# A two-layer GLA / attention / S5 trunk step: layer 1's S5 constants computed during layer 0, and attention's q, k, v passed through DRAM

## The chip, the cores and the metric

The kernel runs on one NeuronCore of one Trainium2 chip. The metric is device time in microseconds for one launch, less is better. TensorE is called PE below, VectorE DVE, ScalarE ACT, GpSimd POOL, and SyncE (which issues the DMAs of this kernel) SP.

## The reference

Two layers run on 640 tokens: 128 context tokens and 512 latent tokens, 1024 channels wide, all in fp32. Each layer has three branches that read the same normalised input: gated linear attention (GLA), latent attention (MLA) and an S5 state-space model. Their outputs are gated, projected, mixed and added to the residual. What matters here is cut from the reference:

```
# S5: the constants depend on weights alone
dt = exp(log_dt); mag = exp(a_re*dt); ab = mag*(cos(a_im*dt) + i sin(a_im*dt))
coef = (ab - 1) / (a_re + i a_im)
ub = coef * einsum('blgp,gnp->blgn', u, b)          # 32 groups, 64 states, 2 directions
x  = complex_linear_scan(ab, ub, x0)
y  = d_skip*u + Re(einsum('blgn,gpn->blgp', x, c))
# MLA: 4 heads, 96 = 64 + 32 rotary
q = rope(rms_norm(rms_norm(cq) @ w_uq));  k = rope(rms_norm(concat(ckv @ w_uk, k_rope)));  v = ckv @ w_uv
latent tokens attend to 256 cached + 512 latent tokens, context tokens to the 128 context tokens
o = softmax(q k^T / sqrt(96)) v
```

## The kernel before, in words

**Products.** Every large product is made of three fp32r matmuls (high x high, high x low, low x high). A weight half of 128x512 comes by DMA into `wraw`, ACT rounds it into `whi` and DVE subtracts to get `wlo` (`half`, L255; the copies are recorded at L227, the subtraction at L236, all matmuls at L245); each of the three tiles has 4 buffers. Projections go to the PSUM tile `pj`, all else to `bank` (4 buffers).

**Order.** PE runs strictly in the order in which the program is written. The other engines and the DMA queue on SP are put in order ahead of time by a scheduler that has a priority for each instruction; at run time each engine follows its own list and waits at the first row that is not ready. So an instruction of low priority, once it has a place in the list, holds back whatever stands behind it.

**Fill.** Projections that nothing waits for yet stand ready as generators in `self.stand`. `fill(n)` takes n steps from them; one step is six matmuls of 320 columns on 128x128 weights (four with `whi`, two with `wlo`). Fill is called where PE would otherwise wait. When `stand` is empty, `fill` does nothing.

**One layer** (`layer`, L1480) runs: S5 kernel, S5 input and `s5_z`, `s5_pow`, `s5_scan`, `s5_y`, `s5_glu`, then `mla_qkv`, `mla_heads`, then GLA, merges and output projection.

**S5's constants.** `s5_prep` (L632) makes from the weights the powers `s5pw`, the input coefficients `s5w` and the step `s5ab`: some 120 small DVE instructions. `s5_kernel` (L732) then makes 16 tiles `s5qk` of 128x512 by `outer` (L712: two products and a sum, recorded at L716, L717 and L718), stores each to DRAM (`qd`, L756) for use in `s5_y` (L947), and multiplies them with `s5rd`; `s5_z` makes 16 tiles `s5r` in the same way (its transposes are at L825); `s5_pow` (L856) doubles the powers in four rounds. Each round of `s5_pow` is followed by four fill steps:

```
for _ in self.s5_pow(p):
    fill(FILL[3])          # FILL[3] = 4
for _ in self.s5_scan(p):
    fill(FILL[3])
```

For layer 1, `s5_prep` and the first parts of `s5_kernel` stand at the end of layer 0 and the start of layer 1.

**Attention.** `mla_qkv` (L1077) makes k in 7 token tiles, v in 7 and q in 5. For each tile of k and q, ACT squares and copies the product out of PSUM, DVE reduces (`hss`), POOL raises to the power -1/2 (`hrs`), DVE scales each of four heads (L1133, L1165) and applies the rotation (L1065 to L1068). The results stay in the SBUF tiles `qt`, `kt`, `vt` for all heads. `mla_heads` (L1169) then transposes a head's part of q and k on PE (`load`, transposes at L1183), splits v (`values`), and runs scores, softmax, transposes of P (L1236) and the product with v for the query groups A and B (256 latent tokens each) and C (the 128 context tokens). The first head's transposes follow `mla_qkv` and ten fill steps.

Of the kernel before, what the change touches and what calls it, by code (L numbers as in the profile page):

```python
# [19 lines left out]
L = 2  # L20
# [164 lines left out]
FILL = (17, 2, 1, 4, 2, 10, 10, 1, 7, 3)  # L185
FM = (1, 6, 1, 4, 2, 4, 3, 2, 1)
# [15 lines left out]
class Prog:  # L202
# [113 lines left out]
    def consts(self):  # L316
# [20 lines left out]
        self.qd = [self.dr.tile([8, 2, 128, 512], F32, name=f"qd{l}") for l in range(L)]  # L337
        self.sud = [self.dr.tile([NT, 512], F32, name=f"sud{l}") for l in range(L)]
# [246 lines left out]
    def cmul(self, V, p, o_r, o_i, ar, ai, br, bi, shape):  # L585
        pat = "p (a b) -> p a b"
        t1 = p.tile([128, shape[1] * shape[2]], F32, name="cm1", tag="cm1")
        t2 = p.tile([128, shape[1] * shape[2]], F32, name="cm2", tag="cm2")
        t1, t2 = (t.rearrange(pat, a=shape[1]) for t in (t1, t2))
# [26 lines left out]
    def exp_(self, V, p, out, x):  # L616

        t = p.tile([128, 3, 64], F32, name="ex", tag="ex")
        k, r, y = t[:, 0], t[:, 1], t[:, 2]
# [8 lines left out]
        e = p.tile([128, 64], I32, name="exi", tag="exi")  # L628
# [3 lines left out]
    def s5_prep(self, l, vec, p, pz, ptmp):  # L632

        V = self.V
        n0 = VEC["B1"][0]
        bs, cs = pz.tile([128, 1024], F32, name="s5b"), p.tile([128, 1024], F32, name="s5c")
        with self.tc.high_priority(5200):
            for i, t in enumerate((bs, cs)):
                self.S.dma_start(t, self.a["vec"][l][:, n0 + 1024 * i:n0 + 1024 * i + 1024])
        self.B1, self.B2, self.C1, self.C2 = (t[:, 512 * i:512 * i + 512].rearrange("p (g c) -> p g c", c=16)  # L640
                                              for t in (bs, cs) for i in range(2))
        are, aim, ldt = vec("are"), vec("aim"), vec("ldt")
        sm = ptmp.tile([128, 11, 64], F32, name="s5sm")
# [33 lines left out]
        pw = p.tile([128, 9, 2, 64], F32, name="s5pw")  # L677
# [32 lines left out]
        self.pw, self.w, self.ab = pw, w, ab  # L710
# [21 lines left out]
    def s5_kernel(self, l, vec, p):  # L732
# [3 lines left out]
        V.tensor_scalar(c0, self.C1, self.nsgn, None, op0=ALU.mult)  # L736
# [6 lines left out]
        for d in range(2):  # L743
            tmp = p.tile([128, 4, 8, 16], F32, name="s5qk0t", tag="s5qk0t", bufs=1)
# [64 lines left out]
    def s5_z(self, p, fill):  # L809
# [5 lines left out]
        def front(b, d):  # L815
            r = p.tile([128, 4, 8, 16], F32, name="s5r", tag=f"s5r{d}", bufs=2 + d)
            tmp = p.tile([128, 4, 8, 16], F32, name="s5rtmp", tag=f"s5rtmp{d}", bufs=1)
# [4 lines left out]
            self.outer(V, p, r, tmp, w[0], w[1], self.B1[:, 4 * b:4 * b + 4], self.B2[:, 4 * b:4 * b + 4], sh)  # L822
            ps = self.bank()
# [32 lines left out]
    def s5_pow(self, p):  # L856

        pt = p.tile([128, 2, NB, 64], F32, name="s5pt")
        V = self.V
        for i in range(2):  # L860
            V.tensor_copy(pt[:, i, 0], self.ab[:, i])
        n = 1
        while n < NB:
            sh = [128, n, 64]
            a, b = (pt[:, i, 0:n] for i in range(2))
            c, d = (pt[:, i, n - 1][:, None, :].to_broadcast(sh) for i in range(2))
            t1 = p.tile([128, NB // 2, 64], F32, name="sp1", tag="sp1")[:, 0:n]
            t2 = p.tile([128, NB // 2, 64], F32, name="sp2", tag="sp2")[:, 0:n]
            o = [pt[:, i, n:2 * n] for i in range(2)]
            V.tensor_tensor(t1, a, c, op=ALU.mult)  # L870
            V.tensor_tensor(t2, b, d, op=ALU.mult)
            V.tensor_tensor(o[0], t1, t2, op=ALU.subtract)
            V.tensor_tensor(t1, a, d, op=ALU.mult)
            V.tensor_tensor(t2, b, c, op=ALU.mult)
            V.tensor_tensor(o[1], t1, t2, op=ALU.add)
            n *= 2
            yield
# [198 lines left out]
    def mla_qkv(self, pa, p):  # L1076
# [42 lines left out]
        for t in range(7):  # L1119
# [16 lines left out]
            if 2 <= t < 6:  # L1136
                self.rope_(p, kt[:, :, 64:96], t - 2)
# [496 lines left out]
```

## Time and profile before

| | |
|---|---|
| runs, us | 1604.42, 1606.25, 1602.03 (median 1604.42) |
| profiled execution, its own time | 1601.22 us |
| its span | 1599.4 us |
| mean granted PE clock | 0.981 |
| PE busy | 1516.4 us (95%) in 11334 matmuls |
| DVE busy | 1056.4 us (66%) in 2435 instructions |
| ACT busy | 631.8 us (40%) |
| POOL busy | 47.7 us (3%) |
| DMA | 179.73 MB, 108792 packets |

The profile is of one execution. An idle time in it is put down to the event that came last before the waiting instruction. The granted clock is given as a share of 2.4 GHz; 0.50 is the lower of its two levels, 1.2 GHz.

### The profile page before, as it was taken

How to read it: one execution, taken by the hardware profiler on the slowest of the kernel's cores; microseconds unless marked ns; L12 is line 12 of the kernel's file. 1: busy time of each engine (PE TensorE's matmuls, PEld its weight loads, DVE VectorE, ACT ScalarE, POOL GpSimd, SP SyncE). 2: the span in 40 equal slices, each digit the busy share in tenths (PEclk: the TensorE clock that was granted, in tenths of full speed). 3: DMA queues.
4: the chain of work that ended last, by engine and by line, in shares of the span. 5: the costliest groups of instructions: out<-in, count | busy, mean ns of one | idle time of the engine just before them, and what ended most of it. 6: DMA issues, size and time to landing. Idle time of an engine off the chain costs nothing. (4 is left out here: it accounts for less than half of the span.)

```text
span 1599.4 us, 28779 instructions
## 1 busy us (share of the span) xinstructions
PE 1516.4 (95%) x11334; PEld 1438.9 (90%) x11334; DVE 1056.4 (66%) x2435; ACT 631.8 (40%) x1171; POOL 47.7 (3%) x48
## 2 busy tenths in 40 slices
PE   4999999999998898999799999999999989989999
PEld 3789999999997888898697999999999979889998
DVE  8986992367566436879987579724766663477762
ACT  3335223555444353333223542244544442634331
POOL 0000000012000000000000000000210000000000
PEclk9999999999999899999899999999999999999999
DMA  9451435323311121227553432442332122212253
GB/s 339 169 152 42 154 114 157 117 86 115 113 55 58 46 75 54 65 85 255 206 193 92 124 112 90 138 151 76 106 120 93 55 66 66 68 60 60 93 166 107
DMA packets 108792, 179.73 MB, mean 112 GB/s; under 512 B 12656, under 2 KB 30768, under 8 KB 108656
## 3 DMA queue, kind: packets, MB, share of 16 engines
q1 hardware_dynamic: 108656, 177.89, 34.3%
q8 instruction: 89, 1.46, 0.4%
q14 instruction: 47, 0.39, 0.1%
HBM read 149.23 MB, written 28.61 MB: 111 GB/s over the span
## 5 line engine op out<-in xcount | busy, mean ns | idle before, releaser
L245 PE MATMUL pj<-h,whi 128*128 128x320 f32 x3456 | 664.1, 313 | 0.0
L245 PEld LDWEIGHTS pj<-h,whi 128*128 128x128 f32 x3456 | 541.2, 189 | 6.6 <-issue 5.1
L227 ACT ACTIVATE whi<-wraw 128x512 fp32r<-128x512 f32 x326 | 205.0, 631 | 508.4 <-PE pj L245 359.2
L245 PE MATMUL pj<-h,wlo 128*128 128x320 f32 x1728 | 397.3, 310 | 0.0
L236 DVE TENSOR_TENSOR wlo<-wraw,whi 128x512 fp32r<-128x512 f32 x326 | 223.9, 688 | 245.5 <-ACT whi L227 238.6
L245 PEld LDWEIGHTS pj<-h,wlo 128*128 128x128 f32 x1728 | 290.3, 188 | 0.0
L245 PE MATMUL pj<-og,whi 128*128 128x320 f32 x736 | 142.1, 313 | 0.3 <-DVE og L236 0.3
L245 PEld LDWEIGHTS pj<-og,whi 128*128 128x128 f32 x736 | 114.7, 188 | 4.7 <-ACT whi L227 1.6
L245 PE MATMUL pj<-whi,h 128*128 128x512 f32 x256 | 87.1, 401 | 6.3 <-ACT h L230 5.7
L245 PE MATMUL pj<-og,wlo 128*128 128x320 f32 x384 | 87.5, 309 | 0.0
L245 PEld LDWEIGHTS pj<-whi,h 128*128 128x128 f32 x256 | 48.7, 192 | 19.5 <-ACT h L230 6.3
L245 PEld LDWEIGHTS pj<-og,wlo 128*128 128x128 f32 x384 | 64.2, 188 | 0.0
L230 ACT ACTIVATE P<-bank,smx 128x384 f32<-128x384 f32 x64 | 36.4, 575 | 56.0 <-DVE smx L1215 56.0
L236 DVE TENSOR_TENSOR Ptl<-bank,Pth 128x512 fp32r<-128x512 f32 x48 | 32.1, 689 | 34.3 <-ACT Pth L227 33.7
L230 ACT ACTIVATE th<-pj 128x640 f32<-128x640 f32 x72 | 49.6, 689 | 5.5 <-PE pj L245 5.4
L245 PE MATMUL pj<-wlo,h 128*128 128x512 f32 x128 | 50.8, 397 | 0.0
L245 PE MATMUL pj<-s5g,whi 128*128 128x320 f32 x256 | 48.1, 310 | 0.0
L245 PE MATMUL bank<-s5qy,mx 128*80 128x128 f32 x256 | 46.1, 302 | 0.0
L227 ACT ACTIVATE Pth<-bank 128x512 fp32r<-128x512 f32 x48 | 27.5, 596 | 41.3 <-PE bank L1236 41.1
L1236 PE MATMUL bank<-c,P 128*128 128x128 f32 x192 | 32.2, 304 | 11.9 <-ACT P L230 5.3
L1211 DVE TENSOR_REDUCE smx<-bank 128x1 f32<-128x384 f32 (+1 forms) x72 | 36.2, 524 | 9.0 <-PE bank L245 8.1
L1400 DVE SCALAR_TENSOR_TENSOR st<-st,bl,bank 64x128 f32<-64x128 f32 x112 | 38.9, 347 | 3.6
(349 smaller groups left out, 2324.2 us busy)
## 6 DMA issues: line engine op xcount, KB each, us to landing
wraw<-wpk SPq DMA_DIRECT2D x358, 256.0 KB, 2.7
og<-wpk SPq DMA_DIRECT2D x48, 256.0 KB, 5.1
qd<-s5qk SPq DMA_DIRECT2D x32, 256.0 KB, 2.2
s5qy<-qd SPq DMA_DIRECT2D x32, 256.0 KB, 4.1
gd<-gt SPq DMA_DIRECT2D x16, 320.0 KB, 2.5
gt<-gd SPq DMA_DIRECT2D x16, 320.0 KB, 3.1
md<-th SPq DMA_DIRECT2D x16, 320.0 KB, 2.3
th<-md SPq DMA_DIRECT2D x16, 320.0 KB, 3.1
```

The lines of the kernel that those rows point to most:

```text
L227: self.A.activation(out, in_, AF.Copy, scale=scale)
L230: self.A.activation(out, in_, f, **kw)
L236: (eng or self.V).tensor_tensor(lo, src, hi.bitcast(F32), op=ALU.subtract)
L245: self.T.matmul(out, lhsT, rhs, start=start, stop=stop, skip_group_check=True, **kw)
L1211: V.tensor_reduce(mx[:, i:i + 1], ps[:, 0:w], axis=AX.X, op=ALU.max)
L1236: self.T.transpose(pt[:, nq * i + 128 * qi:nq * i + 128 * qi + 128], pr[qi][:, 128 * k:128 * k + 128], self.ident)
L1400: V.scalar_tensor_tensor(out, st[r, c, :], bl[r, c:c + 1], pu[c][r], op0=ALU.mult, op1=ALU.add)
```

## The change

- The computation of the S5 constants is moved into `s5_coef`. Layer 0 uses it as before.
- For layer 1 a new function `s5_ahead` computes the constants, the 16 tiles of `s5_kernel`, the 16 tiles of `s5_z` and the powers, and stores them to DRAM (`r0d`, `qd`, `rd`, `ptd`). It is called in layer 0 ahead of `s5_glu` under a priority lowered by 3000. It has one tile of 128x1024 (`s5x`) and four of 128x512 (`s5o`), which `outers` uses in turn: two to a product.
- In layer 1, `s5_prep` is left out, and `s5_kernel`, `s5_z` and `s5_pow` read these results from DRAM.
- `s5_pow` is no generator any more, so in both layers its four rounds of four fill steps are gone; the steps stay in `stand` and are taken later.
- In attention, q, k and v no longer stay in SBUF. Each token tile of k or q is made in the tile `qkt` (two buffers, shared by k and q), each of v in `vts` (two buffers), and stored to DRAM; each head reads its own part back: q and k in pieces of 96 fp32 numbers (384 bytes), v in pieces of 128 (512 bytes).

The diff, cut to its core:

```
+AHEAD = 3000
+    def s5_ahead(self, l, vec, p):
+        V = self.V
+        n0 = VEC["B1"][0]
+        big = lambda: p.tile([128, 1024], F32, name="s5x", tag="s5x", bufs=1)
+        tmp = lambda i=0: p.tile([128, 512], F32, name="s5o", tag="s5o", bufs=4)
+        pw, w = p.tile([128, 9, 2, 64], F32, name="s5pw"), p.tile([128, 8, 2, 64], F32, name="s5w")
+        ab = p.tile([128, 2, 64], F32, name="s5ab")
+        self.s5_coef(vec, pw, w, ab, big().rearrange("p (a b) -> p a b", b=64), tmp)
...
+        def outers(m, coef, dst):
+            for b in range(8):
+                for d in range(2):
+                    o, t = tmp(), tmp()
...
+                    self.outer(V, p, v4(o), v4(t), s[0], s[1], m[0][:, 4 * b:4 * b + 4], m[1][:, 4 * b:4 * b + 4], sh)
+                    self.S.dma_start(dst[b, d], o)
+        C = load(1)
...
+        outers(C, lambda i, g: pw[:, 1:9, i, g], self.qd[l])
+        B = load(0)
...
+        outers(B, lambda i, g: w[:, :, i, g], self.rd[l])
...
+        self.S.dma_start(self.ptd[l][:, :, 0:8], pt)
...
     def s5_kernel(self, l, vec, p):
...
-            q = [self.s5_q(V, p, b, d, f"s5qk{d}", 4) for d in range(2)]
...
+                if l:
+                    q.append(p.tile([128, 4, 8, 16], F32, name=f"s5qk{d}", tag=f"s5qk{d}", bufs=4))
+                    self.S.dma_start(q[d], m)
...
     def s5_z(self, p, fill):
...
+            if self.l:
+                self.S.dma_start(r, self.rd[self.l][b, d].rearrange("p (a b c) -> p a b c", a=4, b=8))
+                return turn(r)
...
     def mla_qkv(self, pa, p):
...
-        self.qt = pa.tile([128, 5, 4, 96], F32, name="qt")
-        self.kt = pa.tile([128, 7, 4, 96], F32, name="kt")
-        self.vt = pa.tile([128, 7, 512], F32, name="vt")
+        mkt = lambda: p.tile([128, 4, 96], F32, name="qkt", tag="qkt", bufs=2)
...
+            self.S.dma_start(self.ktd[l][t].rearrange("p (h x) -> p h x", h=4), kt)
...
+            vt = p.tile([128, 512], F32, name="vts", tag="vts", bufs=2)
...
+            self.S.dma_start(self.qtd[l][t].rearrange("p (h x) -> p h x", h=4), qt)
...
     def mla_heads(self, p):
...
+        def get(h):
+            r = []
+            for nm, n, d in (("qt", 5, self.qtd), ("kt", 7, self.ktd)):
+                r.append(p.tile([128, n, 96], F32, name=nm, tag=nm, bufs=1))
+                self.S.dma_start(r[-1], d[self.l].rearrange("t p (h x) -> p t h x", h=4)[:, :, h, :])
+            return r
...
     def layer(self, l, x):
...
-                    for _ in self.s5_pow(p):
-                        fill(FILL[3])
+                    self.s5_pow(p)
                     for _ in self.s5_scan(p):
                         fill(FILL[3])
...
+            pf = ahead.enter_context(pool("s5f"))
+            if l + 1 < L:
+                with tc.high_priority(-AHEAD):
+                    self.s5_ahead(l + 1, self.nvec, pf)
             with pool("s5b") as p:
                 ogc = self.s5_glu(p, gl, self.gates, fill)
```

Three places show how the change moves instructions.

PE in layer 0, from the scores of head 2's group C to the transposes of head 3's q and k, before: no projection (`pj`) stands there any more, since `stand` is empty.

```order
L245 MATMUL bank<-kTh,qTh 128x128
L245 MATMUL bank<-kTl,qTh 128x128
L245 MATMUL bank<-kTh,qTl 128x128
L1183 MATMUL bank<-c,qt 96x128 x4
L1183 MATMUL bank<-c,kt 96x128 x7
L1183 MATMUL bank<-c,qt 96x128
L1236 MATMUL bank<-c,P 128x128 x8
```

The same place after the change (every `pj<-h,whi` row stands with its `pj<-h,wlo` row for one fill step).

```order
L246 MATMUL bank<-kTh,qTh 128x128
L246 MATMUL bank<-kTl,qTh 128x128
L246 MATMUL bank<-kTh,qTl 128x128
L1272 MATMUL bank<-c,qt 96x128 x4
L1272 MATMUL bank<-c,kt 96x128 x4
L246 MATMUL pj<-h,whi 128x320 x4
L246 MATMUL pj<-h,wlo 128x320 x2
L1272 MATMUL bank<-c,kt 96x128 x3
```

Fill steps now stand between the transposes. All 16 steps taken out before the scan are found here, from the scores of head 2's group B to the scores of head 3's group A; in layer 1 they are found in the scores of head 3's groups A to C. Nothing else on PE moves.

DVE in layer 0, from the last tile of q to the first tiles of attention's first head, before (`vl`, `qTl` and `kTl` are the low halves of v, q and k).

```order
L1165 SCALAR_TENSOR_TENSOR qt<-qt,hrs,rows 128x96 x4
L236 TENSOR_TENSOR vl<-vt,vh 128x896
L236 TENSOR_TENSOR qTl<-bank,qTh 96x512
L236 TENSOR_TENSOR kTl<-bank,kTh 96x512
L236 TENSOR_TENSOR kTl<-bank,kTh 96x384
```

The same place after the change, with the tiles' numbers (`s5o` are the four temporary tiles of `s5_ahead`; L792 and L793 are the products of `outer`, L794 the sum).

```order
L1245 SCALAR_TENSOR_TENSOR qkt_4834<-qkt_4834,hrs_4836,rows_1236 128x96 x4
L793 TENSOR_TENSOR s5o_3673<-s5w_3355,s5x_3604 128x512
L792 TENSOR_TENSOR s5o_3678<-s5w_3355,s5x_3604 128x512
L794 TENSOR_TENSOR s5o_3672<-s5o_3672,s5o_3673 128x512
L793 TENSOR_TENSOR s5o_3679<-s5w_3355,s5x_3604 128x512
L792 TENSOR_TENSOR s5o_3684<-s5w_3355,s5x_3604 128x512
L794 TENSOR_TENSOR s5o_3678<-s5o_3678,s5o_3679 128x512
L793 TENSOR_TENSOR s5o_3685<-s5w_3355,s5x_3604 128x512
L794 TENSOR_TENSOR s5o_3684<-s5o_3684,s5o_3685 128x512
L792 TENSOR_TENSOR s5o_3690<-s5w_3355,s5x_3604 128x512
L237 TENSOR_TENSOR qTl_4938<-bank_4945,qTh_4937 96x512
```

In all, 258 instructions of `s5_ahead` stand on DVE between `s5bq` (the first DVE row of `s5_glu`, L984 before) and the first product of attention's first head (`og`, L1253 before): 114 TENSOR_TENSOR of 128x512, 61 of 128x64, 12 of 128x256, 12 of 128x128, 38 TENSOR_SCALAR of 128x64 and 21 others.

SP in `mla_qkv` of layer 0, before, from the store of the new latents (`ckvo`) on: nearly all are loads of weights.

```order
L1106 DMA ckvo<-ckn 128x128 x2
L1047 DMA gt<-gd_104 128x640
L266 DMA wraw<-wpk 128x512 x20
L357 DMA rows<-row 128x192
L266 DMA wraw<-wpk 128x512 x18
```

And after the change, at the end of `mla_qkv` (`rd1_103` takes the tiles `s5o`, `qtd0_108` those of q).

```order
L745 DMA rd1_103<-s5o_3654 128x512
L1248 DMA qtd0_108<-qkt_4774 128x384
L745 DMA rd1_103<-s5o_3660 128x512
L1248 DMA qtd0_108<-qkt_4804 128x384
L745 DMA rd1_103<-s5o_3666 128x512
L1248 DMA qtd0_108<-qkt_4834 128x384
L364 DMA rows_10071<-row 128x192
L1261 DMA qt_4941<-qtd0_108 128x5x96
L1261 DMA kt_4943<-ktd0_110 128x7x96
L1282 DMA vt_5074<-vtd0_112 128x7x128
L1282 DMA vt_5478<-vtd0_112 128x7x128
L745 DMA rd1_103<-s5o_3672 128x512
```

Stores of `s5_ahead`, stores of q and the reads of the first two heads now stand in one queue, between and ahead of the loads of weights.

## Rows read from the trace of the kernel before

**Rows 1.** The page: span, and busy time of each engine.
```profile
span 1599.4 us, 28779 instructions
PE 1516.4 (95%) x11334; PEld 1438.9 (90%) x11334; DVE 1056.4 (66%) x2435; ACT 631.8 (40%) x1171; POOL 47.7 (3%) x48
```
**Rows 2.** Waits of PE: releaser, us in total, times, longest us.
```profile
PE bank L245 <- DVE s5qk L718: 15.2, 4, 12.2
```
**Rows 3.** Timeline of PE, layer 1's first S5 product: start, us, instruction, [idle before].
```profile
786.04 0.75 PE L245 MATMUL pj<-h,whi 128*128 128x320 f32 x4
...
786.92 0.75 PE L245 MATMUL pj<-h,whi 128*128 128x320 f32 x4
787.51 0.46 PE L245 MATMUL pj<-h,wlo 128*128 128x320 f32 x2
800.16 0.58 PE L245 MATMUL bank<-s5qk,s5rd 128*32 128x112 f32 x2 [12.20 <-DVE s5qk L718]
```
**Rows 4.** Windows: busy us (count) of PE, PEld, DVE, ACT, POOL, PEclk, DMA share, GB/s.
```profile
792.00:804.00 12.00, 3.84 (x36) 3.46 (x37) 11.48 (x20) 1.11 (x2) 0.00 (x0) 0.50 0.74 256
```
**Rows 5.** Timeline of DVE, layer 1's S5 constants.
```profile
762.08 0.22 DVE L693 TENSOR_TENSOR s5sm<-s5sm,vec 128x64 f32<-128x64 f32 x1
762.21 0.22 DVE L598 TENSOR_TENSOR s5pw<-cm,cm 128x64 f32<-128x64 f32 x1
...
784.19 3.09 DVE L716 TENSOR_TENSOR s5qk<-s5pw,s5c 128x512 f32<-128x512 f32 x5
```
**Rows 6.** Timeline, end of the S5 scan on DVE and first use on PE, layer 0.
```profile
243.38 0.65 DVE L934 TENSOR_TENSOR mx<-mx,sf 128x480 f32<-128x480 f32 x1
259.82 0.72 PE L245 MATMUL bank<-s5qy,mx 128*80 128x128 f32 x4
```
**Rows 7.** The same in layer 1.
```profile
1022.39 1.22 DVE L934 TENSOR_TENSOR mx<-mx,sf 128x480 f32<-128x480 f32 x2
1040.70 0.72 PE L245 MATMUL bank<-s5qy,mx 128*80 128x128 f32 x4
```
**Rows 8.** Timeline of PE, attention's last heads of layer 0: first and last of five idle times.
```profile
501.58 0.33 PE L245 MATMUL bank<-kTh,qTh 96*128 96x128 f32 x1 [0.53 <-ACT P L230]
511.93 0.49 PE L245 MATMUL bank<-Pt,vt 128*128 128x128 f32 x2 [1.10 <-ACT Pt L227]
```
**Rows 9.** Timeline of PE, attention's last head of layer 1: five idle times.
```profile
1305.52 0.30 PE L1236 MATMUL bank<-c,P 128*128 128x128 f32 x1 [2.22 <-ACT P L230]
1307.23 1.73 PE L1236 MATMUL bank<-c,P 128*128 128x128 f32 x7 [1.41 <-DVE P L1222]
1318.54 0.48 PE L245 MATMUL bank<-kTh,qTh 96*128 96x128 f32 x1 [3.56 <-ACT P L230]
1320.45 0.45 PE L1236 MATMUL bank<-c,P 128*128 128x128 f32 x1 [1.00 <-DVE smx L1220]
1321.43 1.73 PE L1236 MATMUL bank<-c,P 128*128 128x128 f32 x7 [0.53 <-DVE smx L1221]
```
**Rows 10.** Windows over the two stretches there that follow the longer idle times.
```profile
1307.20:1310.50 3.30, 3.27 (x15) 3.00 (x16) 1.39 (x2) 1.19 (x2) 0.00 (x0) 0.52 0.00 0
1318.50:1327.40 8.90, 7.32 (x31) 6.61 (x32) 4.49 (x13) 3.92 (x11) 0.00 (x0) 0.50 0.21 53
```
**Rows 11.** Window from `s5bq` to attention's first `og`, layer 0.
```profile
296.99:419.69 122.70, 122.27 (x848) 115.32 (x848) 73.34 (x197) 60.71 (x112) 16.68 (x14) 1.00 0.31 101
```
**Rows 12.** DMA issues: count, KB each, median us from issue to landing.
```profile
qd<-s5qk SPq DMA_DIRECT2D x32, 256.0 KB, 2.2
s5qy<-qd SPq DMA_DIRECT2D x32, 256.0 KB, 4.1
...
s5b<-vec SPq DMA_DIRECT2D x2, 512.0 KB, 5.4
```
**Rows 13.** Timeline of ACT, DVE and PE around layer 1's q tiles.
```profile
1162.87 0.57 ACT L227 ACTIVATE qt<-bank,rsm 128x384 f32<-128x384 f32 x1
1168.38 0.28 DVE L1068 TENSOR_TENSOR qt<-rp,rp 128x128 f32<-128x128 f32 x1
1176.45 1.00 DVE L1165 SCALAR_TENSOR_TENSOR qt<-qt,hrs,rows 128x96 f32<-128x96 f32 x4
1177.21 0.60 PE L1183 MATMUL bank<-c,qt 128*96 128x128 f32 x4
```

More of the change, by code (lines that the diff above doesn't have):

```diff
@@ L337, in consts @@
         self.qd = [self.dr.tile([8, 2, 128, 512], F32, name=f"qd{l}") for l in range(L)]
+        self.rd = [self.dr.tile([8, 2, 128, 512], F32, name=f"rd{l}") for l in range(L)]
+        self.r0d = [self.dr.tile([3, 128, 512], F32, name=f"r0d{l}") for l in range(L)]
+        self.ptd = [self.dr.tile([128, 2, NB, 64], F32, name=f"ptd{l}") for l in range(L)]
+        self.qtd = [self.dr.tile([5, 128, 384], F32, name=f"qtd{l}") for l in range(L)]
+        self.ktd = [self.dr.tile([7, 128, 384], F32, name=f"ktd{l}") for l in range(L)]
+        self.vtd = [self.dr.tile([7, 128, 512], F32, name=f"vtd{l}") for l in range(L)]
         self.sud = [self.dr.tile([NT, 512], F32, name=f"sud{l}") for l in range(L)]
@@ L614, in poly, with exp_ @@
             V.tensor_scalar(out, out, c, None, op0=ALU.add)
-    def exp_(self, V, p, out, x):
-        t = p.tile([128, 3, 64], F32, name="ex", tag="ex")
-        k, r, y = t[:, 0], t[:, 1], t[:, 2]
+    def exp_(self, V, sm, out, x):
+        k, r, y = (sm[:, i] for i in (11, 12, 13))
         V.tensor_scalar(r, x, -87.0, 88.0, op0=ALU.max, op1=ALU.min)
@@ L627, in exp_, with s5_coef @@
         V.tensor_scalar(k, k, 127.0, 8388608.0, op0=ALU.add, op1=ALU.mult)
-        e = p.tile([128, 64], I32, name="exi", tag="exi")
+        e = sm[:, 14].bitcast(I32)
         V.tensor_copy(e, k)
         V.tensor_tensor(out, y, e.bitcast(F32), op=ALU.mult)
-    def s5_prep(self, l, vec, p, pz, ptmp):
+    def s5_coef(self, vec, pw, w, ab, sm, tmp):
         V = self.V
[L635 to L641, printed above, removed]
         are, aim, ldt = vec("are"), vec("aim"), vec("ldt")
-        sm = ptmp.tile([128, 11, 64], F32, name="s5sm")
         dt, tre, th, kk = (sm[:, i] for i in range(4))
@@ L709, in s5_prep @@
         V.tensor_scalar(pw[:, 1:9, 1], pw[:, 1:9, 1], -1.0, None, op0=ALU.mult)
-        self.pw, self.w, self.ab = pw, w, ab
+    def s5_prep(self, l, vec, p, pz, ptmp):
+        n0 = VEC["B1"][0]
+        bs, cs = pz.tile([128, 1024], F32, name="s5b"), p.tile([128, 1024], F32, name="s5c")
+        with self.tc.high_priority(5200):
+            for i, t in enumerate((bs, cs)):
+                self.S.dma_start(t, self.a["vec"][l][:, n0 + 1024 * i:n0 + 1024 * i + 1024])
+        self.B1, self.B2, self.C1, self.C2 = (t[:, 512 * i:512 * i + 512].rearrange("p (g c) -> p g c", c=16)
+                                              for t in (bs, cs) for i in range(2))
+        sm = ptmp.tile([128, 16, 64], F32, name="s5sm")
+        self.pw = p.tile([128, 9, 2, 64], F32, name="s5pw")
+        self.w = pz.tile([128, 8, 2, 64], F32, name="s5w")
+        self.ab = p.tile([128, 2, 64], F32, name="s5ab")
+        self.s5_coef(vec, self.pw, self.w, self.ab, sm,
+                     lambda i: ptmp.tile([128, 512], F32, name=f"cm{i}", tag=f"cm{i}"))
@@ new lines, in powers @@
+    def powers(self, pt, at, ab, tmp):
+        V = self.V
+        for i in range(2):
+            V.tensor_copy(at(i, 0, 1)[:, 0], ab[:, i])
+        n = 1
+        while n < NB:
+            sh = [128, n, 64]
+            a, b = (at(i, 0, n) for i in range(2))
+            c, d = (at(i, n - 1, n).to_broadcast(sh) for i in range(2))
+            t1, t2 = tmp(n), tmp(n)
+            o = [at(i, n, 2 * n) for i in range(2)]
+            V.tensor_tensor(t1, a, c, op=ALU.mult)
+            V.tensor_tensor(t2, b, d, op=ALU.mult)
+            V.tensor_tensor(o[0], t1, t2, op=ALU.subtract)
+            V.tensor_tensor(t1, a, d, op=ALU.mult)
+            V.tensor_tensor(t2, b, c, op=ALU.mult)
+            V.tensor_tensor(o[1], t1, t2, op=ALU.add)
+            n *= 2
@@ L858, in s5_pow @@
         pt = p.tile([128, 2, NB, 64], F32, name="s5pt")
[L859 to L877, printed above, removed]
+        if self.l:
+            self.S.dma_start(pt, self.ptd[self.l])
+        else:
+            self.powers(pt, lambda i, lo, hi: pt[:, i, lo:hi], self.ab,
+                        lambda n: p.tile([128, 512], F32, name="sp", tag="sp", bufs=2)[:, 0:64 * n].rearrange("p (e x) -> p e x", x=64))
         self.pt = pt
@@ L1474, in s5_open @@
         vec = self.nvec if l else self.vec
-        with self.pool_("s5p", l) as p:
-            self.s5_prep(l, vec, pa, pz, p)
+        if not l:
+            with self.pool_("s5p", l) as p:
+                self.s5_prep(l, vec, pa, pz, p)
         pk = ExitStack()
@@ L1552, in layer @@
         ek.close()
+        ahead = ExitStack()
         with ExitStack() as eg:
@@ L1577, in layer @@
                 ogb = self.mla_heads(p)
+        ahead.close()
         self.stand = [g for g in self.stand if g is not early] + [self.finish_tile(early)]
```

87 lines of the change are left out of this document (62 added, 25 removed).

## The prediction, made before the changed kernel was run

> **What bounds the kernel now.** I read the page first [rows 1]: PE is busy 95% of the span, DVE 66%. So a microsecond counts only where PE has no work or waits, and the average of DVE says little; it has to be read stage by stage. Then the list of PE's waits [rows 2]: its largest entry is DVE's S5 tiles, 15.2 us, 12.2 of them in one piece. The timeline shows where [rows 3]: at the start of layer 1 PE has used up its fill at about 788 and stands until 800.16. Last come windows over the stretch into which the work is moved [rows 11]: there PE is busy 122.27 of 122.70 us and DVE 73.34, so DVE has 49.4 us free. The prediction hangs on whether the new DVE work fits into these.
>
> All of the sum is made against the profiled execution, 1601.22 us, which is 3.2 us below the median of the runs, 1604.42.
>
> **Layer 1's first wait goes: -14.1 us.** PE's 12.20 us are spent behind DVE, which makes the `s5qk` tiles and the rest of the preparation [rows 3]. They are no longer computed there. With them goes what the clock cost: in 792 to 804 the granted clock is 0.50, its lower level, after PE had been idle, and PE works 3.84 us in it [rows 4], half of which, 1.9, is lost. The ends are -14.1 and 0: the latter if reading the tiles back takes the place of making them.
>
> **Fill moved out of the way of the scan: nothing lost there.** Per layer 16 fill steps leave, each 0.88 us (two starts in [rows 3]), 14.1 us in all. PE then comes to the first product behind the scan that much earlier. In layer 0 DVE ends the scan at 244.03 and PE needs it at 259.82, 15.8 us later [rows 6]; 1.7 us of that cover are left. In layer 1 it is 1023.61 and 1040.70, 17.1 us [rows 7]. So no new wait, but if DVE came 3 us later in layer 0, PE would stand there for 1.3. That layer 1 has less DVE work in `s5_z` and `s5_pow` I cost at nothing, for the same cover hides it already.
>
> **The same steps come back at the end of attention: -3.2 and -10 us.** There `stand` was empty. In layer 0 five idle times between 501.58 and 511.93 [rows 8] sum to 3.2 us (0.53, 0.42, 0.39, 0.72 and 1.10); the 16 steps now lie over them and are used up by the scores of head 3's group A, ahead of the later idle times. In layer 1 they lie over five idle times of 2.22, 1.41, 3.56, 1.00 and 0.53 us, 8.7 together [rows 9]; and behind two of them PE worked 3.27 us at a clock of 0.52 and 7.32 at 0.50 [rows 10], which lost 1.6 and 3.7. I take the idle time and a quarter of the clock's, -10; the ends are -3.6 (the first two alone) and -14.0 (all).
>
> **The new DVE work in layer 0: +53 us.** 258 instructions go between `s5bq` and the first `og`. On DVE, instructions in a row start closer than they last: five of 128x512 take 3.09 us, so 0.60 each after the first's 0.69, and two of 128x64 start 0.13 apart [rows 5]. On the line through these two sizes 256 elements cost 0.33 and 128 cost 0.20. That makes 114 x 0.60 = 68.4, 61 x 0.13 = 7.9, 12 x 0.33 = 4.0, 12 x 0.20 = 2.4, 38 x 0.13 = 4.9, and 21 others at about 0.2, 4.2: 92 us. The 73.3 us that DVE has there already [rows 11] shrink to some 68 if packed, by the 0.09 us that the distance is below the duration where now a gap follows. Together 160 us for a stretch of 122.7: **37 too many**. No matter how low the priority was, DVE goes through its list in order, and k's, v's, q's and softmax's instructions stand behind and between these.
>
> On top come waits for the stores. `s5o` has four buffers, two to a product, so a product waits until the tile of the last but one has landed in DRAM. A store of the same size lands after 2.2 us [rows 12]. In the order shown, one instruction (0.6 us) stands between the sum of `s5o_3672` and the first product of `s5o_3684`, which takes its buffer: 1.6 us of waiting. Going through the whole list so, 17 products wait, 15.3 us in all. The two loads of `s5x` wait for its single buffer too and land after 5.4 us [rows 12] with some 4 to 5 us of other instructions in between, 1 or 2 us; PE, which may be a few banks ahead when the stretch ends, gives back about as much. So 37 + 15 = 53 (unrounded). The ends: 37 if stores never hold DVE; 91 if each takes the 4.1 us that a read takes [rows 12] in this fuller queue (by the same walk, 53.6 us of waiting).
>
> The Trainium skill, page "DMA: Bandwidth & Descriptors", section "Anatomy of one DMA — SWDGE (gpsimd) path", gives a fit of about 2.0 us plus the bytes over 436 GB/s, 2.6 us for 256 KB; by it the walk gives some 22 us in place of 15. The row, on this kernel's own queue and for this very transfer, says 2.2, and I go by the row.
>
> **q, k, v through DRAM.** In layer 0 this lies within the stretch just costed, where DVE has other rows to do; nothing is added, and without that cover it would be as in layer 1: **+11 us**. There the transposes began at 1177.21, right behind the last scaling of q at 1176.45 to 1177.45 [rows 13], so there is no slack. With two buffers a tile's copy waits for the store of the tile two before. From q's first copy, 1162.87, to the end of its rotation, 1168.66, it is 5.8 us; with the store, 8.0. The fifth tile's copy can then begin at 1162.87 + 2 x 8.0 = 1178.9; about 3 us for copy, reduction and scaling, 2.2 for the store and 4.1 for the read [rows 12] put the transposes at 1188.2. The ends are 5 (a tile takes 3 us less where DVE is free) and 15 (k's last tiles push q's first by 4 us). Ten fill steps ahead of them are already where they were.
>
> **Sum:** -14.1 - 3.2 - 10 + 53 + 11 = +36.7. Profiled 1637.9, and with 3.2 for the median **1641 us**. The bytes added are no bound: the DMA engines are busy 0.31 of that stretch [rows 11].
>
> **The rivals.**
>
> *DVE's free time hides the work (faster).* DVE is 66% busy [rows 1] and has 49.4 us free there [rows 11]. If PE lost nothing, the sum would be -14.1 - 3.2 - 10 + 11 = -16.3: 1588 us. It decides at one point: whether DVE needs more than 122.7 us from `s5bq` to `og`. Against it stands 160. Chance 0.06.
>
> *Stores and buffers cost nothing.* Only the 37 us of excess work remain, and 5 in layer 1: +14.7, 1619 us. For it: DVE's list may have other rows where I see waits. Chance 0.17.
>
> *SP holds the stores back.* Reads of q and k stand in front of stores of `s5o`, and wait for the last store of q; loads of weights wait for their buffers. With 3.0 us a store the walk gives 30 us, the stretch 67 and the time 1655; with 4.1 it is 1679. For it: one queue has it all. Against: it is mostly filled in the order in which DVE works. Chance 0.15.
>
> *The first wait does not go.* PE then waits at layer 1's start for reads of `qd` in place of DVE: the change does not do what it says, +14.1, 1655 us. Against: the results lie in DRAM some 300 us earlier, and four buffers a direction can be filled ahead. Chance 0.10.
>
> *Small pieces are slow.* If reads of q and k in 384-byte pieces take twice the 4.1 us, head 0's transposes come 4.1 us later in each layer: +8, 1649 us. Nothing in the rows shows a read of that kind. Chance 0.12. The Trainium skill, page "DMA: Bandwidth & Descriptors", section "Specifications", speaks for this: line rate wants pieces of at least 512 B, below which the engine reads, modifies and writes.
>
> **How the numbers follow.** My own case has 0.40. A measurement of this kernel can tell about 0.3%, 4.8 us, from no change. Slower by more than that are all but the first rival and a small part of the second: 0.89; within it 0.04; faster 0.07. The range 1608 to 1670 leaves out the first rival and the far end of the third; its low end is the second rival with the larger gains in the tails, its high end a stretch that costs some 80 us.
>
> **What would show it.** Right: PE's 12.2 us wait on `s5qk` is gone and layer 1's attention tail has fewer idle times; the time from `s5bq` to the first `og` grows from 123 to about 175 us with DVE busy nearly throughout, waits of `s5o` on stores sum to some 15 us, and layer 1's first transposes of q wait about 11 us for a DMA. Wrong: if DVE has idle time left in that stretch and PE none, the first rival holds; if PE waits there for weights rather than for DVE, it is the queue.

## The result and the profile after

| | before | changed |
|---|---|---|
| median of the runs, us | 1605.34 (4 runs) | 1656.12 (4 runs, 1654.16 to 1657.68) |
| ratio, 95% interval | | 1.032 [1.030, 1.034] |
| span of the profiled execution, us | 1599.4 | 1655.3 |
| mean granted PE clock | 0.981 | 0.966 |

The change makes the kernel slower by 50.8 us in the median, by 55.9 us between the two profiled spans. The page of the changed kernel stands beside [rows 1]:

```profile
span 1655.3 us, 29092 instructions
...
PE 1529.5 (92%) x11334; PEld 1449.8 (88%) x11334; DVE 1057.4 (64%) x2435; ACT 636.3 (38%) x1171; POOL 64.9 (4%) x48
...
DMA packets 142585, 212.78 MB, mean 129 GB/s; under 512 B 26864, under 2 KB 55216, under 8 KB 142320
```

PE has the same 11334 matmuls, and DVE the same instructions and the same busy time; they have only been moved. PE is busy 13 us longer for them, at a lower mean clock, and idle for the rest of the loss. POOL is busy 17 us longer with the same 48 instructions. The list of PE's waits of the changed kernel (releaser, us in total, times, longest us) says for what it now stands; [rows 2] is its first line before. (The lines of the program have moved: matmuls are now recorded at L246, the transposes of q and k at L1272, those of P at L1327. `cch` is the high half of the cached latents, from which the first tiles of k and v are made.)

```profile
PE bank L1272 <- DMA qt<-qtd: 28.3, 2, 19.8
...
PE bank L246 <- ACT qkt L228: 13.7, 5, 6.5
...
PE bank L1327 <- DVE P L1313: 8.5, 5, 3.7
PE bank L246 <- DVE mx L1013: 7.6, 1, 7.6
PE bank L246 <- ACT cch L228: 5.8, 1, 5.8
...
PE bank L246 <- DVE s5qk L794: 3.9, 3, 1.9
...
PE bank L1327 <- DVE s5o L780: 2.0, 1, 2.0
```

The 12.2 us for `s5qk` are gone. New are the read of q (19.8 us in layer 0, 8.5 in layer 1), the copies of the k and q tiles, `cch`, and `mx`, which is the scan of layer 1.

Where the time went is read by taking the same PE instruction in both traces and following by how much later it starts. The steps between such points add up to the 55.9 us but for 0.1 (fill that only moved within a layer is taken out):

| part | predicted | measured |
|---|---|---|
| layer 0, `s5bq` to the end of attention's first head | +53 | +56.8 |
| layer 0, attention's tail | -3.2 | -6.1 |
| layer 1, first S5 product | -14.1 | -14.6 |
| layer 1, scan, and the slower clock and small rows behind it | 0 | +11.4 |
| layer 1, q, k, v through DRAM | +11 | +17.4 |
| layer 1, attention's tail | -10 | -9.3 |
| small remainders: +1.6 ahead of `s5bq`, -1.4 behind layer 0's attention | 0 | +0.2 |
| sum | +36.7 | +55.8 |

Two rows of the idle times that remain in layer 1's tail answer to the five of [rows 9]:

```profile
1376.45 0.30 PE L1327 MATMUL bank<-c,P 128*128 128x128 f32 x1 [1.88 <-DVE P L1313]
1377.98 1.73 PE L1327 MATMUL bank<-c,P 128*128 128x128 f32 x7 [1.23 <-DVE P L1313]
```

The window over the stretch of [rows 11], from `s5bq` to the first `og`, in the changed kernel:

```profile
284.50:464.00 179.50, 136.29 (x848) 125.14 (x848) 163.50 (x456) 62.87 (x112) 34.23 (x14) 0.86 0.49 164
```

It is 179.5 us long instead of 122.7 with the same 848 matmuls on PE; DVE is busy 163.5 of it (160 were predicted) and has 259 more instructions. So the size was foreseen well. But what was said to make it up was not right, as DVE's waits for stores in that window show (all there are, and the load of `s5x`):

```profile
DVE s5o L755 <- DMA s5x<-vec: 2.0, 1, 2.0
...
DVE s5o L781 <- DMA rd<-s5o: 1.0, 1, 1.0
...
DVE s5o L792 <- DMA rd<-s5o: 0.7, 1, 0.7
```

1.7 us, not 15.3. The timeline of DVE shows why, and shows also how the early rows stand among those of layer 0's q:

```profile
417.71 0.32 DVE L1245 SCALAR_TENSOR_TENSOR qkt<-qkt,hrs,rows 128x96 f32<-128x96 f32 x1
417.94 0.17 DVE L1151 TENSOR_SCALAR hrs<-hss 128x4 f32<-128x4 f32 x1
418.01 0.69 DVE L793 TENSOR_TENSOR s5o<-s5w,s5x 128x512 f32<-128x512 f32 x1
418.61 0.69 DVE L792 TENSOR_TENSOR s5o<-s5w,s5x 128x512 f32<-128x512 f32 x1
...
423.49 1.00 DVE L1245 SCALAR_TENSOR_TENSOR qkt<-qkt,hrs,rows 128x96 f32<-128x96 f32 x4 [0.90 <-POOL hrs L243]
...
425.61 0.68 DVE L794 TENSOR_TENSOR s5o<-s5o 128x512 f32<-128x512 f32 x1
426.22 0.68 DVE L793 TENSOR_TENSOR s5o<-s5w,s5x 128x512 f32<-128x512 f32 x1
426.82 0.68 DVE L792 TENSOR_TENSOR s5o<-s5w,s5x 128x512 f32<-128x512 f32 x1
427.42 0.68 DVE L794 TENSOR_TENSOR s5o<-s5o 128x512 f32<-128x512 f32 x1
428.14 0.69 DVE L793 TENSOR_TENSOR s5o<-s5w,s5x 128x512 f32<-128x512 f32 x1
```

SP issues the next stores of such tiles only afterwards:

```profile
429.67 2.22 SPq L745 DMA_DIRECT2D rd<-s5o  x3
```

The products (L792, L793) at 426.82 and 428.14 run on although the sums (L794) that end at 426.29 and 428.10 are not yet on their way. A product does not always take "the tile of the last but one": whichever of the four tiles is free is taken, and the tile of a product's second term is free as soon as the sum is made.

The other half of these rows is POOL. Between `hrs` at 417.94 and the scaling at 423.49 lies one power -1/2 of 128x4 elements on POOL, and it lasts 5.20 us. POOL's groups in 280 to 470 us, before and then in the changed kernel (busy us, mean ns, idle before):

```profile
L242 POOL TENSOR_TENSOR hrs<-hrs,c 128x4 f32<-128x4 f32 x12 | 13.8, 1159 | 57.9 <-DVE hrs L1072 57.9
```
```profile
L243 POOL TENSOR_TENSOR hrs<-hrs,c 128x4 f32<-128x4 f32 x12 | 24.5, 2042 | 79.4 <-DVE hrs L1151 79.4
L243 POOL TENSOR_TENSOR rsm<-rsm,c 128x5 f32<-128x5 f32 x2 | 9.8, 4888 | 288.5 <-DVE rsm L433 288.5
```

### The profile page after: what moved, and what is told of

Same layout as the page of the kernel before. It is cut to its first block, busy times and chain, and to the rows that moved or that the text cites. A ratio compares the mean times of both kernels' runs of the same rounds, so it can differ in the third digit from the quotient of the medians.

```text
span 1655.3 us, 29092 instructions
## 1 busy us (share of the span) xinstructions
PE 1529.5 (92%) x11334; PEld 1449.8 (88%) x11334; DVE 1057.4 (64%) x2435; ACT 636.3 (38%) x1171; POOL 64.9 (4%) x48
## 5 line engine op out<-in xcount | busy, mean ns | idle before, releaser
L246 PE MATMUL pj<-h,whi 128*128 128x320 f32 x3456 | 669.0, 315 | 0.4 <-DVE gt L492 0.4
L246 PEld LDWEIGHTS pj<-h,whi 128*128 128x128 f32 x3456 | 544.7, 190 | 7.1 <-issue 4.8
L246 PE MATMUL pj<-h,wlo 128*128 128x320 f32 x1728 | 399.2, 311 | 0.0
L246 PEld LDWEIGHTS pj<-h,wlo 128*128 128x128 f32 x1728 | 292.4, 190 | 0.0
L246 PE MATMUL pj<-og,whi 128*128 128x320 f32 x736 | 141.8, 313 | 0.0
L246 PEld LDWEIGHTS pj<-og,whi 128*128 128x128 f32 x736 | 114.7, 188 | 4.2 <-ACT whi L228 1.6
L246 PE MATMUL pj<-whi,h 128*128 128x512 f32 x256 | 86.3, 398 | 5.4 <-ACT h L231 4.7
L246 PE MATMUL pj<-og,wlo 128*128 128x320 f32 x384 | 87.6, 309 | 0.0
L246 PEld LDWEIGHTS pj<-og,wlo 128*128 128x128 f32 x384 | 64.1, 188 | 0.2 <-DVE wlo L237 0.2
L246 PEld LDWEIGHTS pj<-whi,h 128*128 128x128 f32 x256 | 48.8, 191 | 17.6 <-ACT h L231 5.4
L246 PE MATMUL bank<-s5qy,mx 128*80 128x128 f32 x256 | 47.1, 308 | 7.6 <-DVE mx L1013 7.6
L246 PE MATMUL pj<-wlo,h 128*128 128x512 f32 x128 | 50.6, 395 | 0.0
L246 PE MATMUL pj<-s5g,whi 128*128 128x320 f32 x256 | 49.1, 315 | 0.0
L246 PEld LDWEIGHTS bank<-s5qy,mx 128*80 128x80 f32 x256 | 41.2, 230 | 8.0 <-DVE mx L1013 8.0
L246 PE MATMUL bank<-whi,cqk 128*128 128x384 f32 (+2 forms) x140 | 39.1, 349 | 7.5 <-ACT qkt L228 7.5
L1327 PE MATMUL bank<-c,P 128*128 128x128 f32 x192 | 31.4, 303 | 14.4 <-DVE P L1313 8.5
L581 DVE SCALAR_TENSOR_TENSOR mx<-pj,ada,tmp 128x320 f32<-128x320 f32 (+2 forms) x48 | 18.1, 433 | 41.4 <-PE pj L246 39.2
```

The lines of the kernel that those rows point to most:

```text
L246: self.T.matmul(out, lhsT, rhs, start=start, stop=stop, skip_group_check=True, **kw)
L581: V.scalar_tensor_tensor(xn[:, j, lo:hi], ps[:, i, lo - 320 * i:hi - 320 * i], self.ads[l, 2][r][:, j:j + 1], xr[:, lo:hi], op0=ALU.mult, ...
L1327: self.T.transpose(pt[:, nq * i + 128 * qi:nq * i + 128 * qi + 128], pr[qi][:, 128 * k:128 * k + 128], self.ident)
```

## The experiments

My theory after the result: layer 0 loses (a) DVE's excess, some 37 us, and (b) the way of q, k and v through DRAM, which I had thought hidden; layer 1 loses (b) again and a new wait at the scan. The rival for (a) is that early rows cost by where they stand, in front of rows that PE is soon waiting for, and not only by the excess over DVE's free time.

**1. The filler change alone, on the kernel before.**

```
 for _ in self.s5_pow(p):
-    fill(FILL[3])
+    pass
```

> The kernel before, with one edit: the four rounds of the powers no longer call fill, so 16 fill steps per layer go to the end of attention; S5 of layer 1 and q, k, v are as before. My theory (the steps pay where PE stood idle, and the scan still ends about 3 us ahead of PE in layer 1): -6.7 us in layer 0 and -10 in layer 1, as the aligned traces of before and after show for these places, 1588 us. Rival (the cover is needed: with the powers' rounds on DVE the scan comes late, as layer 1's did by 7.6 us in the changed kernel): a wait of about 5 to 8 us in front of layer 1's first S5 output product, 1594 to 1597 us.

Measured: 1587.21 us, ratio 0.989 [0.987, 0.992]. As expected: the tails' gain is real, and no scan waits. In the stretch of [rows 11] this kernel loses 2.4 us, whose cause I leave open. This small part of the change by itself is faster than the kernel before.

**2. The filler and q, k, v through DRAM, nothing early.**

```
-if l:
+if False:
...
-if not l:
...
-with tc.high_priority(-AHEAD):
-    self.s5_ahead(l + 1, self.nvec, pf)
```

> The changed kernel without the early computation: layer 1 makes its S5 constants as before; the fill steps are moved and q, k, v go through DRAM. My theory (the 53 to 57 us lost in layer 0's stretch come from DVE's extra instructions; the path through two buffers and DRAM costs what it cost in layer 1, about 17 us, in each layer, now that nothing hides it in layer 0): 16 us below before from the fill, 34 above, 1623 us, and layer 0's stretch some 17 us longer than before, not 57. Rival (the loss in layer 0's stretch is the path through DRAM and the queue, not DVE's work): the stretch stays 50 us longer and the time is 1650 or more.

(The first pair stands at five places, in the S5 kernel, `s5_z` and `s5_pow`; layer 1 computes all as layer 0 does.) Measured: 1624.72 us, 1.014 [1.011, 1.017]; 37.5 us behind experiment 1, 18.5 of it in layer 0 and the rest in layer 1. The stretch of [rows 11] is now:

```profile
284.10:427.40 143.30, 127.66 (x848) 118.80 (x848) 74.70 (x197) 62.07 (x112) 16.80 (x14) 0.94 0.41 129
```

DVE has no more work than before (74.70 us for 73.34), and yet the stretch is 20.6 us longer. So in layer 0 the way through DRAM is no more hidden than in layer 1. The early rows then add 36 us from 143.3 to 179.5. So of the 56.8 us that the stretch loses in all, 2.4 stand in experiment 1 already, 18.3 are the way through DRAM and 36.2 the early rows. The last is close to the 37 us of excess that I had forecast, which made the excess look like the whole law. Experiments 5 and 8 test that.

**3. The changed kernel, with the read of the scan's powers early.**

```
-self.S.dma_start(pt, self.ptd[self.l])
+with self.tc.high_priority(6000):
+    self.S.dma_start(pt, self.ptd[self.l])
```

> The changed kernel with one edit: the read of layer 1's powers from DRAM has a higher priority, so that it stands on SP ahead of the reads for the S5 output and not behind them. My theory (the scan of layer 1 started 20 us late because that one transfer of 1 MB was issued at 989.6 behind others and landed 7.7 us later): the wait of 7.6 us in front of the first S5 output product and the slow clock behind it go, 9 to 10 us less than the changed kernel, 1646 us. Rival (DVE's own rows set the scan's end): the wait stays, 1656 us.

Measured: 1650.43 us, 5.7 us faster than the changed kernel, less than expected; the wait at the scan is gone. By the same PE rows in the two traces this place gives 9.1 us back. In the changed kernel this read stands on SP's queue behind the reads of `s5m` and `s5qy`, and lands after DVE wants it. Three rows, of SP, DVE and PE:

```profile
989.59 0.65 SPq L953 DMA_DIRECT2D s5pt<-ptd  x1
997.31 0.49 DVE L975 TENSOR_TENSOR sc<-mx,s5pt 128x320 f32<-128x320 f32 x1 [2.51 <-DMA s5pt<-ptd]
1070.77 0.51 PE L246 MATMUL bank<-s5qy,mx 128*80 128x128 f32 x1 [7.59 <-DVE mx L1013]
```

**4. The changed kernel, with five buffers for the rows of k and q instead of two.**

```
-name="qkt", tag="qkt", bufs=2)
+name="qkt", tag="qkt", bufs=5)
```

> The changed kernel with one edit: the token tiles of k and q have five buffers in place of two. My theory (two buffers make each copy wait for the store of the tile two before): in layer 1 the waits of 4.0 us ahead of v and 0.8 in q go and of the 8.5 ahead of the transposes some 5 to 6 stay (last store 2.2 and read 3 to 4), in all 7 to 8 us less than the changed kernel there and 0 to 4 in layer 0, where DVE is the limit: 1645 to 1649 us. Rival (it is the last store and the read alone): 1656 us.

Measured: 1638.45 us, 17.7 us faster, more than expected: some 12 of it in layer 0, where 0 to 4 were expected, and 7 in layer 1. In the changed kernel ACT shows the two buffers at work, here for layer 1's q:

```profile
1204.33 0.57 ACT L228 ACTIVATE qkt<-bank,rsm 128x384 f32<-128x384 f32 x1
1205.26 0.59 ACT L228 ACTIVATE qkt<-bank,rsm 128x384 f32<-128x384 f32 x1
...
1214.15 0.59 ACT L228 ACTIVATE qkt<-bank,rsm 128x384 f32<-128x384 f32 x1 [5.13 <-DMA qtd<-qkt]
```

**5. Half of the early rows** (the constants and the 16 tiles of the S5 kernel: by the trace 184 of the 258 instructions, some 56 of the 92 us; the input tiles and the scan's powers are computed in layer 1 as before).

```
-outers(B, lambda i, g: w[:, :, i, g], self.rd[l])
...
+self.S.dma_start(self.wd, w)
+self.S.dma_start(self.abd, ab)
```

> The changed kernel with a smaller early part: only the constants, the tiles of the S5 kernel and what goes with them (172 of the 258 DVE instructions, 56 us by the same prices in place of 92) are made in layer 0; the tiles of s5_z and the powers are made in layer 1 as before. My theory (early work costs by what it exceeds of DVE's free time in the stretch; with q, k, v through DRAM alone the stretch lasts 143 us and DVE has some 70 us free in it): 56 us fit, 0 to 10 us are lost by order, and layer 1's first wait of 12 to 14 us is still gone: 1624.7 - 13.9 + 5 = 1616 us, range 1611 to 1621. Rival (every microsecond of early work on DVE costs PE in proportion, 38 us for 92): 23 us lost, 1634 us.

Measured: 1631.64 us, 1.017 [1.014, 1.019]. The rival is nearer. The stretch:

```profile
285.90:447.80 161.90, 134.90 (x848) 124.46 (x848) 127.95 (x382) 62.00 (x112) 26.02 (x14) 0.91 0.49 156
```

The stretch of experiment 2 had room for these rows: 127.95 us of DVE's work in 143.3. Still it became 18.6 us longer, with DVE idle for 34. So it is not the excess that counts: each us of early rows cost about 0.33 us here (18.6 of 56) and 0.39 with all of them (36 of 92).

**6. The constants alone early** (by the trace 129 instructions), on experiment 1, between layer 0's attention and GLA.

```
+with self.pool_("s5e", l + 1) as pe, tc.high_priority(-1000):
+    self.s5_coefs(self.nvec, pe, pe, pe)
+    for t, d in ((self.pw, self.pwd), (self.w, self.wd), (self.ab, self.abd)):
+        self.S.dma_start(d, t)
```

> The kernel before with the fill steps moved (as in e1) and one edit more: of layer 1's S5 only the constants (powers, coefficients, step; some 120 small DVE instructions, about 22 us) are made early, in the merge between attention and GLA of layer 0, where DVE is busy 19 of 60 us, and go through DRAM; q, k and v stay in SBUF. My theory (the 12.2 us wait at layer 1's start is DVE's backlog, and 22 us less of it just there end it; DVE's free time in the merge hides the work): 12 to 14 us below e1, 1573 to 1576 us. Rival (the wait is set by the S5 tiles, not by the constants, or the early work holds back the merge): no gain, 1585 to 1590 us.

Measured: 1596.43 us (11 runs), 0.996 [0.994, 0.997], 9 us behind experiment 1. Neither was right. Layer 1's wait is gone (`s5qk` from 16.0 us to 3.4), but a new one has come:

```profile
PE pj L245 <- ACT gqt L227: 14.8, 1, 14.8
```

My reading: GLA's tiles take the memory of the early ones, and so wait until the early rows, which have a low priority, are through. Experiment 11 tests it.

**7. Experiments 3 and 4 together**, on the changed kernel.

```
+with self.tc.high_priority(6000):
+    self.S.dma_start(pt, self.ptd[self.l])
...
+name="qkt", tag="qkt", bufs=5)
```

> The changed kernel with both mends, the early read of the powers (e3) and five buffers for k and q (e4). My theory (the two losses lie in different places and add up): 1656 - 17.7 - 5.7 = 1633 us. Rival (the one takes up what the other frees, since a scan that ends late is in the path of both): 1637 us or more.

Measured: 1628.13 us, 1.015 [1.013, 1.017], 28.0 us faster than the changed kernel, where the parts by themselves give 5.7 + 17.7. By the spans of the profiled executions they add up: 27.6 us for 8.0 + 19.3. The repaired change is still slower than the kernel before.

**8. Experiment 5 with five buffers.**

```
-name="qkt", tag="qkt", bufs=2)
+name="qkt", tag="qkt", bufs=5)
```

> e5 with five buffers for the token tiles of k and q. My theory (the stretch in layer 0 shrinks by what the path through two buffers costs until DVE's work fills it; 68 + 56 = 124 us of DVE work are less than its 130): 1616 - 17 = 1599 us, range 1593 to 1608. Rival (with the shorter stretch DVE's early work becomes the limit again): 8 to 10 us more, 1609 us.

Measured: 1614.49 us, 17.1 us faster than experiment 5, but 15 above what the excess theory gives.

**9. Experiment 2 with five buffers**, by the same edit.

> q, k and v through DRAM, nothing of the S5 kernel early, and now five buffers for the rows of q and k instead of two. Theory (each layer pays about 17 to 20 us for the way through DRAM, of which the chain through two buffers is 12 us in layer 0 and 7 in layer 1, as the run with five buffers and all early rows showed): 1624.7 - 17 to 19 = 1606 to 1608 us; layer 0 is then some 5 us behind the kernel with only the filler change and layer 1 some 13. Rival (the two buffers cost layer 0 its 12 us only because VectorE was full of early rows; without them the buffers are worth the 7 us a layer that layer 1 showed): 1624.7 - 14 = 1610 to 1612 us.

Measured: 1614.29 us, 10.4 us faster than experiment 2: nearer to the rival, and short of it too. In layer 0 the buffers alone are worth 4.6 us, not 12; the rest comes where DVE is full. What stays is the way itself (`qt<-qtd`, both layers, longest in layer 0):

```profile
PE bank L1272 <- DMA qt<-qtd: 17.1, 2, 9.2
```

8 to 9 us a layer are the last tile's copy, store and read. Some 5 us more in each layer are small shifts in front of q whose cause I leave open. Against this kernel, experiment 4 shows what all the early rows cost with five buffers: 28 us by the end of layer 0's attention.

**10. Experiment 8, with the early rows held behind layer 0's q**, so that they fall into the attention heads.

```
+self.lastq = V.scalar_tensor_tensor(qt[:, h], qt[:, h], rs[:, h:h + 1], ...).ins
...
+with tc.high_priority(-AHEAD), tc.issue_after(self.lastq):
+    self.s5_ahead(l + 1, self.nvec, pf)
```

> The constants and the 16 tiles of the S5 kernel early (172 VectorE instructions, some 56 us), five buffers, as in the run of 1614.5 us, but VectorE may take them only behind the last scaling of q in layer 0, so that they stand in the attention heads, where VectorE has some 77 us free in 170, and not among the chains of k, v and q. Theory (the early rows cost what they do because they stand in front of those chains, and because POOL's power slows beside them; the heads give PE several products between two results of VectorE): the loss of 15 to 20 us in layer 0 goes, 1597 to 1601 us, and POOL's hrs comes back under 1.3 us each. Rival (early rows cost 0.35 us per us wherever PE waits for VectorE, in the heads through the maximum and the softmax's scaling): 1612 to 1617 us.

Measured: 1619.98 us, 1.010 [1.006, 1.013]: slower by 5.5 us than experiment 8, beyond even the rival. The first half of the theory holds: the transposes of q come 14.5 us earlier, and POOL's `hrs` is back at its time of before (1161 ns). But the heads lose 25 us. A window of the heads in experiment 8, then in this one, and two of PE's seven idle times between 415 and 480 here:

```profile
430.00:480.00 50.00, 50.00 (x368) 48.73 (x367) 29.85 (x72) 22.37 (x51) 0.00 (x0) 1.00 0.36 108
```
```profile
430.00:480.00 50.00, 39.80 (x247) 37.33 (x246) 48.05 (x105) 17.92 (x41) 0.00 (x0) 0.88 0.55 178
```
```profile
420.05 1.22 PE L1323 MATMUL bank<-c,P 128*128 128x128 f32 x7 [3.29 <-DVE P L1309]
450.26 0.98 PE L1323 MATMUL bank<-c,P 128*128 128x128 f32 x7 [3.22 <-DVE P L1309]
```

The held rows are not spread over the free time of the heads; they come as a block as soon as they may, fill DVE (48 of 50 us) and stand in front of the softmax; behind PE's idle times its granted clock is lower too (0.88 in this window).

**11. Experiment 6 with the early tiles on the other side of SBUF.**

```
-with self.pool_("s5e", l + 1) as pe, tc.high_priority(-1000):
+with self.pool_("s5e", l + 1, side="right") as pe, tc.high_priority(-1000):
```

> The kernel with only the filler change, and the constants of layer 1 (66 VectorE instructions) computed between layer 0's attention and its gated linear attention, as in the run of 1596.4 us, but with their tiles on the other side of SBUF, so that the tiles of the gated linear attention do not take their memory. Theory (that run lost 15 us at the wait for gqt, which was the wait for this memory): the wait goes, and of the 12.8 us gained at layer 1's entry 10 to 13 are left: 1574 to 1578 us. Rival (the 66 rows hold up the merge wherever their tiles lie): 1585 to 1597 us, with PE waiting over 8 us somewhere between 560 and 620 us.

Measured: 1582.53 us, 0.986 [0.983, 0.990]: the fastest of all, 23 us ahead of the kernel before, of which experiment 1 alone has 17. No wait for `gqt` is left, which shows that it was one for memory. The span is 5.8 us shorter than experiment 1's: layer 1's entry gains 14.1, but by then the kernel is 8.3 behind; part of that lies where PE waits for `og` behind DVE (2.15 us at 725.65, 0.26 in experiment 1). By their medians the two kernels differ by 4.7 us, about what can be told apart.

## Why the prediction was right in size and wrong in a part of its reasons

**Right.** *Layer 1's first wait*: -14.6 for -14.1; the tiles read back take no place of it. *The tails*: in layer 1 -9.3 for -10; in layer 0 -6.1 for -3.2, and experiment 1, with the fill steps alone, shows -7.1 at the same place. PE's idle time there falls from 13.0 to 9.6 us, which is the term; the rest is in PE's busy time, and its cause stays open. The two windows, before and then changed:

```profile
494.60:540.07 45.47, 32.46 (x182) 27.49 (x180) 28.36 (x74) 19.73 (x50) 0.00 (x0) 0.85 0.10 34
```
```profile
538.90:592.30 53.40, 43.82 (x278) 41.12 (x276) 31.53 (x78) 23.52 (x56) 1.24 (x3) 0.87 0.18 60
```

*The amount of DVE work* and the length of the stretch: 163.5 us for 160, 179.5 us for about 175. *The rivals*: experiment 5 speaks against the first beyond its own terms, for free time does not hide the work even where there is enough. Of the second, the half on the stores was right: they cost next to nothing, and its 1619 us are missed because q, k and v are not hidden in layer 0. The third did not show: stores of `rd` do land after 3.0 us in the median, as it had them, but in that stretch DVE waits 1.7 us for them in all and PE 0.3 us for weights. For small pieces, `qt<-qtd` lands 240 KB in 3.6 us where `s5qk<-qd`, 256 KB in pieces of 2 KB, takes 3.6 as well (two other such reads, `s5r<-rd` and `s5qy<-qd`, take 2.9 and 4.0):

```profile
s5qk<-qd SPq DMA_DIRECT2D x16, 256.0 KB, 3.6
...
qt<-qtd SPq DMA_DIRECT2D x8, 240.0 KB, 3.6
```

The rule of the Trainium skill, page "DMA: Bandwidth & Descriptors", section "Specifications", that pieces under 512 B miss line rate, does not show in these landings.

**Wrong, and cancelling: layer 0's +53.** The step "17 products wait, 15.3 us in all" fell: 1.7 us were measured, because a tile is taken when it is free and not in turn. The step "in layer 0 this lies within the stretch just costed ... nothing is added" fell too: experiment 2 has +18.3 there with no early row at all. One error is some 14 us too much and the other 18 too little: that the sum came out near 53 is luck. The step "37 too many" gave the right number (36 to 38 between experiment 2 and the changed kernel), but not for the reason given: experiment 5 loses 18.6 us there with 34 us of DVE's time free. The rows cost where they stand in front of a result for which PE has nothing else to do. In order of the list these are `cch`, k's and q's scaling (with their store and read), and the softmax.

**Wrong: "that layer 1 has less DVE work in `s5_z` and `s5_pow` I cost at nothing".** I looked at the cover of the scan (17.1 us, [rows 7]) but not at what releases its start. With the change that is a 1 MB read on the one queue, behind all that layer 1 reads before it. Fill left the same place by 14.1 us, so the cover was nearly used up, and PE stood for 7.6 us; behind it the clock was lower (0.83 in 1071 to 1080). Experiment 3 gives 5.7 us of the 11.4 back by the medians, 9.1 by the rows.

**Undersized: layer 1's +11 for q, k, v.** Measured +17.4. For q alone the term was rather too large: from its first copy to the transposes I had worked out 25.3 us, before it was 14.3 [rows 13], and it is 22.1 (1204.33 to 1226.46), so +7.8. But k's seven tiles go through the same two buffers, and q's first copy comes 41.5 us later than before, where the stage ahead of k had been 33.7 late: another 7.8. I had 4 us of that, and only in the upper end of the term. The rest, 1.8, comes behind the transposes of q: PE hardly waits any more, but from 1226.4 to 1232, after 8.5 us of standing, its granted clock is 0.58. Experiment 4 gets 7 of this back.

**In all**, of the 19 us between the forecast profile and the measured one, 11.4 are the scan and its sequel, 6.4 the way of q, k and v in layer 1, 3.8 layer 0's stretch, and -2.5 the tails and small terms. What stays open: the split of the early rows' cost into POOL's slowness, DVE's places and the buffers was not made one by one, since they are not additive (the buffers are worth some 12 us in layer 0 with all early rows, experiment 4, and 4.6 without any, experiment 9).

## What to carry to other kernels

Work moved to an engine with free time is not free at low priority: on an engine that runs a list in order, the rows come in a block as early as they can, and each us of them cost here 0.24 to 0.41 us of PE (experiments 8 and 10, against 9) wherever they stood in front of a short chain. Look for the rows that PE is waiting for, not at the busy share; where the moved work is small (129 rows, experiment 11) and its tiles take no one's memory, it may pay: 4.7 us by the medians, about what can be told apart. The larger gain here, 17 us, came from fill steps moved to where PE stood idle (experiment 1). When a computed value becomes a read, ask what stands before that read on its queue and with how many buffers its source goes out.

## What the runs showed of the hardware that was not expected

One small power on POOL (128x4) took 1.16 us in the mean before, 1.60 in experiment 5 and 2.04 in the changed kernel; one of 128x5 took 8.10 us:

```profile
309.54 1.68 POOL L243 TENSOR_TENSOR rsm<-rsm,c 128x5 f32<-128x5 f32 x1 [288.24 <-DVE rsm L433]
311.52 8.10 POOL L243 TENSOR_TENSOR rsm<-rsm,c 128x5 f32<-128x5 f32 x1 [0.30 <-DVE rsm L433]
```

It slows where DVE runs one TENSOR_TENSOR (a product or sum of two tiles) after another, and is at its old time in experiment 10, 1.16 us, where the same rows run after POOL's last power. Rows of SCALAR_TENSOR_TENSOR, which read two tiles as well, did not slow it. Before, two powers took 1.99 us, the second beside four such rows:

```profile
384.78 1.99 POOL L242 TENSOR_TENSOR hrs<-hrs,c 128x4 f32<-128x4 f32 x2 [13.72 <-DVE hrs L1072]
385.83 1.01 DVE L1165 SCALAR_TENSOR_TENSOR qt<-qt,hrs,rows 128x96 f32<-128x96 f32 x4 [0.38 <-POOL hrs L242]
```

The Trainium skill, page "GPSIMD Engine Reference", section "Specifications", says that POOL shares its SBUF interfaces with VectorE and that DVE instructions with two SBUF inputs contend with it; the trace agrees for the TENSOR_TENSOR rows and gives the price, but not for the others. Each tile of k and q passes through POOL, so this lies in the chain PE waits for.
